# Taking both parts of x as one 512-column operand in two of three expert blocks, and more error parts by adding transfers

## The chip, the cores and the metric

The kernel runs on one core of a Trainium2 chip. The metric is the device time of one execution in microseconds (us). The kernel before was run three times: 2606.54, 2606.63 and 2608.71 us, median 2606.63 us.

## The reference

The reference is a small network on 256 tokens of width 1024 in f32: an mLSTM layer and a latent-attention layer, each followed by a PEER layer, and then a block of two feed-forward layers around a mixing layer. The change lies in PEER, which stands twice in the network:

```python
def peer_ffn(x, w_q, sub_keys, u, v):
    q = (xt @ w_q).reshape(T, PEER_HEADS, 2, PEER_HALF)
    s = jnp.einsum('thcd,hcnd->thcn', q, sub_keys)
    s1, i1 = lax.top_k(s[:, :, 0], K); s2, i2 = lax.top_k(s[:, :, 1], K)
    ...                                     # the best 16 of the 256 sums, for each of 8 heads
    gates = jax.nn.softmax(top_s, axis=-1)
    ub = jnp.take(u, eb, axis=0)            # 16,384 experts of width 1024
    act = jax.nn.gelu(jnp.einsum('thkd,td->thk', ub, xb), approximate=False)
    vb = jnp.take(v, eb, axis=0)
    return jnp.einsum('thk,thkd->td', gb * act, vb)
```

The kernel does not gather. It computes gelu(u x) for all 16,384 experts and all tokens, multiplies with a gate matrix that is zero for the experts not chosen, and multiplies the product with v.

## The kernel before, in words

Precision. Each f32 operand of a matrix product is kept as two parts in a narrower format of TensorE: `hi` is the rounded value, `lo` what is left over. A product is three products: hi·hi, hi·lo and lo·hi. For the activations the two parts are `self.xT[0]` and `self.xT[1]`, two halves of one tile of 128 x 2 x 8 x 256 (partition, part, chunk of the width, token), made by `new_xT` (line 459).

Weights come as units of 128 x 1024 f32 (512 KB) in a fixed order, through `Stream`. `load` (line 265) fetches a unit into one of three raw buffers on SP's queue. `prep` (line 284) casts it on ScalarE into `hi` (line 449, or 295) and subtracts on VectorE to get `lo` (line 450). For the units named in `on_dma`, VectorE is spared: `begin` (line 301) lets ScalarE write -w, rounded to the narrower format (line 306), and a transfer of GpSimd's queue then adds w from memory to it (line 307), which leaves `lo`; `spare` gives two buffers in turn for that. Outside the stretch with lent buffers `begin` of unit i is issued while block i-3 is. `fill` (line 310) runs ahead of the products by three units.

PEER. After 16 units for the queries, the 128 expert blocks of a layer follow (`block`, line 940). Block b takes one unit of u: `cols_late` (line 494) issues 16 matmuls with the hi weights, 8 chunks times the two parts of x, and then 8 with the lo weights and x's hi part, all of 256 columns into one PSUM accumulator (four buffers). While block b is issued, `activate` (line 1047) is called for block b-1: ScalarE applies Gelu from PSUM, in two pieces: the tokens whose gates are already joined go to a side buffer (line 1053) and are multiplied in by VectorE (`joins`, line 1061), the other tokens go straight into `big` (line 1056).

Up to block 43 of each layer VectorE works beside the blocks at the selection of the experts. Behind that `Gates` takes over: it spreads 67 steps over the blocks that are left (`upto`, line 1704). A step makes one-hot rows on VectorE (lines 1667, 1668, 1671), TensorE multiplies them (16 matmuls for every two steps, line 1680), and VectorE multiplies the product into `big` in two instructions (lines 1691 and 1693).

Order. VectorE's instructions in this stretch stand in the order in which the code issues them (`in_order`); in block b that is: the lo part of unit b+2, the step, the joins of block b-2. The order on the other engines is set by the scheduler of the framework, with data dependencies and in most places the order of the code; line 306 is held in program order. Each layer lends four more raw buffers to the first 44 expert units (`SELECT`, line 925).

Of the kernel before, what the change touches and what calls it, by code (L numbers as in the profile page):

```python
# [14 lines left out]
AF = mybir.ActivationFunctionType  # L15
ALU = mybir.AluOpType
AX = mybir.AxisListType.X
PSUM = bass.MemoryType.PSUM

P = 128  # L20
D = 1024
S = 256
NT = S // P
KC = D // P
# [17 lines left out]
SELECT, LENT = 44, 4  # L42
# [312 lines left out]
class Net:  # L355
# [96 lines left out]
    def mm(self, ps, a, b, start, stop):  # L452

        mm = self.nc.tensor.matmul
        mm(ps, a[0], b[0], start=start, stop=False)  # L455
        mm(ps, a[0], b[1], start=False, stop=False)  # L456
        mm(ps, a[1], b[0], start=False, stop=stop)  # L457

    def new_xT(self, pool=None, tag="xT", chunks=KC, bufs=1):
        pool = pool or self.gp  # L460
        t = self.t(pool, [P, 2, chunks, S], tag, F32R, bufs=bufs)
        return t[:, 0], t[:, 1]

    def transpose_split(self, src, xT, ti, c0, n):
# [28 lines left out]
    def cols_late(self, ps, xT, unit):  # L493

        mm = self.nc.tensor.matmul
        w = [u.rearrange("p (k c) -> p k c", k=KC) for u in unit]
        steps = [(0, k, part) for k in range(KC) for part in range(2)] + [(1, k, 0) for k in range(KC)]
        for n, (of, k, part) in enumerate(steps):
            mm(ps[:, :S], w[of][:, k], xT[part][:, k], start=n == 0, stop=n == len(steps) - 1)  # L499

    def rows(self, xT, nk=KC, done=None, before=False, then=None):

        acc = self.acc()
        n = nk - self.w.rings[1].size if done else nk
        if done:
            self.w.tail_at(self.w.i + nk)
        if before:
            self.rows_head(acc, xT)
        if then:
            then()  # L510
        for k in range(TAIL if before else 0, n):
            self.rows_k(acc, xT, k, self.w.next(), k == 0, k == nk - 1)
        if done:
            self.rows_tail(acc, [(xT, k) for k in range(n, nk)], n == 0, done)
        return acc
# [371 lines left out]
    def peer(self, layer, gain):  # L887
        nc, v, tc = self.nc, self.nc.vector, self.tc
        mm = nc.tensor.matmul
        with tc.tile_pool(name="pr", bufs=1) as pool:  # L890
            big = self.t(pool, [P, P, S], "big")
# [19 lines left out]

            first = self.w.i + 16
            self.w.lend([self.room(big, n) for n in range(14, 14 + LENT)], range(first, first + SELECT))
            self.w.on_dma = set(range(self.w.i + 16 + 1, self.w.i + 16 + P - 8, 3))

            sc = self.scores_of(big)
            st = {}
# [20 lines left out]
            now, late = {"last": None, "start": None}, []  # L938

            def block(b):  # L940
                ps = self.pp.tile([P, 512], F32, tag="acc", name=self.nm("ub"), bufs=4)
                self.cols_late(ps, self.xT, self.w.next())
                gates, start = now["gates"], now["start"]
                if start is not None:
                    gates.upto(b - 1, Gates.STEPS / (P - 2 - start))
                elif spend(steps, 1.6):
                    inner.close()
                    gates.pool = inner.enter_context(tc.tile_pool(name="gt", bufs=1))
                    now["start"] = b
                if b == P - 2:  # L950
                    gates.rest(b - 1)
                self.joins(late)
                if now["last"]:
                    self.activate(big, gates, late, *now["last"])
                now["last"] = b, ps

            def s_first(i):
                s_query(i) if i < 16 else block(i - 16)
# [11 lines left out]
            with self.in_order():  # L970
                skew([s_first, lambda i: None, s_second], 18)
                for b in range(2, P):
                    block(b)
            gates = now["gates"]
# [69 lines left out]
    def scores_of(self, big):  # L1044
        return big[:, P - 16:, :].rearrange("p b t -> p (b t)").rearrange("p (i h n) -> p i h n", i=NT, h=16)

    def activate(self, big, gates, late, b, ps):

        nc = self.nc
        t0 = gates.tokens if gates else 0  # L1050
        if t0:
            y = self.t(gates.pool, [P, S], "gl") if b % 2 else gates.room
            nc.scalar.activation(y[:, :t0], ps[:, :t0], AF.Gelu)
            late.append((big[:, b, :t0], y[:, :t0]))
        if t0 < S:
            nc.scalar.activation(big[:, b, t0:], ps[:, t0:S], AF.Gelu)  # L1056

    def joins(self, late):
        while late:
# [660 lines left out]
def spend(steps, budget):  # L1720

    while budget > 0:
        c = next(steps, False)
        if c is False:
            return True
        if c is None:
            return False
        budget -= c
    return False
# [59 lines left out]
```

## Time and profile before

| | us |
|---|---|
| median of three runs | 2606.63 |
| the profiled execution, its own time | 2605.68 |
| its span, first to last instruction | 2603.9 |
| TensorE busy in the span | 2545.4 (98%) |
| VectorE busy | 1777.1 (68%) |
| ScalarE busy | 1311.4 (50%) |
| GpSimd busy | 259.7 (10%) |

The two PEER layers run their expert blocks at about 213 to 623 us and 1183 to 1592 us of the span. A matmul's busy time overlaps with that of the next; the pace of a sequence is read from the starts.

### The profile page before, as it was taken

The page shows a single profiled execution, that of the slowest core. Times are in us where ns is not written, and L with a number is a line of the kernel's source. Part 1 is how long each engine was busy: PE and PEld are TensorE (multiplying, and loading weights), DVE is VectorE, ACT ScalarE, POOL GpSimd, SP SyncE. Part 2 cuts the span into 40 slices and gives each one's busy share as a digit, 9 for nine tenths or more (in the row PEclk, how much of TensorE's full clock was granted, in tenths as well). Part 3 has the DMA queues.
Part 4 walks back from the last instruction along what each step waited for, and adds up shares of the span by engine and source line. Part 5 has one row for each costly group of instructions (what it writes and reads, how often), then busy time and mean ns, then how long its engine had stood idle before and what let it go on. Part 6 is the DMA issues. An engine that isn't in the chain of part 4 may idle for free. (4 is left out here: it accounts for less than half of the span.)

```text
span 2603.9 us, 42855 instructions
## 1 busy us (share of the span) xinstructions
PE 2545.4 (98%) x16706; PEld 2300.9 (88%) x16706; DVE 1777.1 (68%) x3244; ACT 1311.4 (50%) x1981; POOL 259.7 (10%) x227
## 2 busy tenths in 40 slices
PE   8999999999999998999999999999999999999999
PEld 6889999999888887889999998888878998987898
DVE  5878977787555567679977776555566547675654
ACT  4445555554444445546555554444445445564543
POOL 0562000000000003010000000000011003101000
PEclk9999999999999999999999999999999999999999
DMA  6357777786555565357877776555566645554653
GB/s 240 118 187 203 216 206 218 211 216 214 194 194 194 194 201 167 116 197 212 225 204 215 211 217 211 193 194 193 194 199 198 218 161 176 171 177 154 210 195 105
DMA packets 139195, 502.42 MB, mean 193 GB/s; under 512 B 15832, under 2 KB 16088, under 8 KB 138992
## 3 DMA queue, kind: packets, MB, share of 16 engines
q1 hardware_dynamic: 122832, 443.93, 51.0%
q0 software_dynamic: 15440, 54.64, 10.8%
q8 instruction: 131, 2.15, 0.3%
q10 hardware_dynamic: 720, 1.11, 0.1%
q14 instruction: 72, 0.59, 0.1%
HBM read 494.38 MB, written 5.24 MB: 192 GB/s over the span
## 5 line engine op out<-in xcount | busy, mean ns | idle before, releaser
L449 ACT CAST whi<-wraw 128x1024 fp32r<-128x1024 f32 x488 | 510.1, 1047 | 689.7 <-PE acc L556 312.3
L450 DVE TENSOR_TENSOR wlo<-wraw,whi 128x1024 fp32r<-128x1024 f32 x446 | 546.9, 1227 | 445.3 <-ACT whi L449 444.3
L499 PE MATMUL ub<-xT,whi 128*128 128x256 f32 x4096 | 538.1, 284 | 0.0
L556 PE MATMUL acc<-whi,xT 128*128 128x512 f32 x1816 | 510.3, 394 | 12.8 <-ACT whi L449 7.3
L499 PEld LDWEIGHTS ub<-xT,whi 128*128 128x128 f32 x4096 | 508.3, 191 | 0.0
L556 PEld LDWEIGHTS acc<-whi,xT 128*128 128x128 f32 x1816 | 342.5, 190 | 86.6 <-ACT xT L449 7.7
L450 DVE TENSOR_TENSOR morelo<-wraw,morehi 128x1024 fp32r<-128x1024 f32 (+1 forms) x214 | 261.7, 1227 | 118.8 <-ACT morehi L449 118.4
L449 ACT CAST morehi<-wraw 128x1024 fp32r<-128x1024 f32 (+1 forms) x227 | 236.8, 1047 | 183.2 <-DMA wraw<-in_wst 72.5
L556 PE MATMUL acc<-wlo,xT 128*128 128x512 f32 x908 | 284.1, 393 | 0.2 <-DVE wlo L450 0.2
L556 PE MATMUL acc<-morehi,xT 128*128 128x512 f32 x808 | 233.9, 390 | 0.0
L499 PE MATMUL ub<-xT,wlo 128*128 128x256 f32 x1408 | 200.1, 285 | 8.6 <-DVE wlo L450 8.1
L556 PEld LDWEIGHTS acc<-wlo,xT 128*128 128x128 f32 x908 | 172.8, 190 | 37.3 <-DVE wlo L450 0.9
L499 PEld LDWEIGHTS ub<-xT,wlo 128*128 128x128 f32 x1408 | 180.9, 191 | 13.4 <-DVE wlo L450 13.1
L556 PEld LDWEIGHTS acc<-morehi,xT 128*128 128x128 f32 x808 | 151.2, 188 | 31.4 <-ACT morehi L449 0.5
L450 POOL TENSOR_TENSOR wlo<-wraw,whi 128x1024 fp32r<-128x1024 f32 (+1 forms) x42 | 100.7, 2400 | 707.0 <-ACT whi L449 702.0
L455 PE MATMUL ps<-xT,whi 128*128 128x256 f32 (+1 forms) x552 | 159.1, 289 | 0.0
L456 PE MATMUL ps<-xT,whi 128*128 128x256 f32 (+1 forms) x552 | 157.4, 285 | 0.4 <-DVE xT L450 0.4
L457 PE MATMUL ps<-xT,wlo 128*128 128x256 f32 (+1 forms) x552 | 157.0, 285 | 0.0
L307 POOL DMA_DIRECT2D x<-in_wst x80 | 69.0, 863 | 735.3 <-ACT big L1056 246.4
L556 PE MATMUL acc<-morelo,xT 128*128 128x512 f32 x404 | 128.3, 390 | 0.8 <-DVE morelo L450 0.8
L457 PE MATMUL ps<-xT,morelo 128*128 128x256 f32 x416 | 118.6, 285 | 1.9 <-POOL morelo L450 1.7
L456 PE MATMUL ps<-xT,morehi 128*128 128x256 f32 x416 | 118.4, 285 | 0.0
(498 smaller groups left out, 4160.0 us busy)
## 6 DMA issues: line engine op xcount, KB each, us to landing
wraw<-in_wst SPq DMA_DIRECT2D x768, 512.0 KB, 4.0
x<-in_wst POOLq DMA_DIRECT2D x80, 512.0 KB, 7.2
big<-in_wst SPq DMA_DIRECT2D x48, 512.0 KB, 5.4
wraw<-in_wst SPq DMA_DIRECT2D x10, 384.0 KB, 3.4
sp<-x SPq DMA_DIRECT2D x4, 512.0 KB, 3.0
big<-in_keys POOLq DMA_DIRECT2D x8, 256.0 KB, 7.0
sp<-big SPq DMA_DIRECT2D x4, 512.0 KB, 8.1
x<-sp POOLq DMA_DIRECT2D x4, 512.0 KB, 3.9
```

The source lines that it names most:

```text
L307: k.nc.gpsimd.dma_start(out=lo[:, :w], in_=self.src[i, :, :w], accum_op=ALU.add)
L449: self.nc.scalar.copy(hi, src)
L450: (self.nc.gpsimd if pool else self.nc.vector).tensor_tensor(lo, src, hi.bitcast(F32), op=ALU.subtract)
L455: mm(ps, a[0], b[0], start=start, stop=False)
L456: mm(ps, a[0], b[1], start=False, stop=False)
L457: mm(ps, a[1], b[0], start=False, stop=stop)
L499: mm(ps[:, :S], w[of][:, k], xT[part][:, k], start=n == 0, stop=n == len(steps) - 1)
L556: mm(acc[ti][h], a, w[b][:, h * 512:(h + 1) * 512], start=first, stop=last)
```

## The change

In blocks beside the gates (`start is not None`) whose number is no multiple of three, `cols_both` takes both parts of x for a chunk as one moving operand of 2 x 256 columns: 8 matmuls of 512 columns with the hi weights, then the 8 of 256 columns with the lo weights. The accumulator then holds hi·hi + lo·hi in its first 256 columns and hi·lo in the other 256. VectorE adds the halves with a reduction over an axis of two, into the place where Gelu's result will stand, and ScalarE's Gelu works in place there. The set `on_dma` keeps every third unit in the first 44 and names every second one from there to unit 118.

```diff
     def new_xT(self, pool=None, tag="xT", chunks=KC, bufs=1):
         ...
+        if tag == "xT":
+            self.both = t
         return t[:, 0], t[:, 1]
+    def cols_both(self, ps, unit):
+        mm = self.nc.tensor.matmul
+        w = [u.rearrange("p (k c) -> p k c", k=KC) for u in unit]
+        for k in range(KC):
+            mm(ps, w[0][:, k], self.both[:, :, k], start=k == 0, stop=False)
+        for k in range(KC):
+            mm(ps[:, :S], w[1][:, k], self.xT[0][:, k], start=False, stop=k == KC - 1)
...
-            self.w.on_dma = set(range(self.w.i + 16 + 1, self.w.i + 16 + P - 8, 3))
+            self.w.on_dma = set(range(first + 1, first + SELECT, 3)) | set(range(first + SELECT, first + P - 8, 2))
...
-                self.cols_late(ps, self.xT, self.w.next())
                 gates, start = now["gates"], now["start"]
+                both = start is not None and b % 3 != 0
+                if both:
+                    self.cols_both(ps, self.w.next())
+                else:
+                    self.cols_late(ps, self.xT, self.w.next())
...
-                now["last"] = b, ps
+                now["last"] = b, ps, both
...
-    def activate(self, big, gates, late, b, ps):
+    def activate(self, big, gates, late, b, ps, both):
         nc = self.nc
         t0 = gates.tokens if gates else 0
+        def gelu(dst, t):
+            src = ps[:, t]
+            if both:
+                src = dst
+                nc.vector.tensor_reduce(dst, ps.rearrange("p (a t) -> p t a", a=2)[:, t], axis=AX, op=ALU.add)
+            nc.scalar.activation(dst, src, AF.Gelu)
         if t0:
             y = self.t(gates.pool, [P, S], "gl") if b % 2 else gates.room
-            nc.scalar.activation(y[:, :t0], ps[:, :t0], AF.Gelu)
+            gelu(y[:, :t0], slice(0, t0))
             late.append((big[:, b, :t0], y[:, :t0]))
         if t0 < S:
-            nc.scalar.activation(big[:, b, t0:], ps[:, t0:S], AF.Gelu)
+            gelu(big[:, b, t0:], slice(t0, S))
```

## Rows read from the trace of the kernel before

**Rows 1.** Windows: busy us per engine, granted clock, DMA share, GB/s; selection, gates.

```profile
214.00:362.00 148.00, 143.76 (x1184) 141.34 (x1184) 134.95 (x407) 87.72 (x129) 12.94 (x15) 1.00 0.77 212
362.00:592.00 230.00, 228.62 (x2128) 227.18 (x2126) 173.72 (x341) 122.91 (x231) 19.89 (x23) 1.00 0.80 217
```

**Rows 2.** TensorE's waits in 214 to 362 us: total, times, longest.

```profile
PE ub L499 <- DVE wlo L450: 4.0, 8, 0.7
```

**Rows 3.** Timeline of TensorE beside the gates: start us, us, engine, line, operation.

```profile
464.18 2.08 PE L499 MATMUL ub<-xT,whi 128*128 128x256 f32 x16
466.10 1.12 PE L499 MATMUL ub<-xT,x 128*128 128x256 f32 x8
...
475.70 1.12 PE L499 MATMUL ub<-xT,x 128*128 128x256 f32 x8
...
591.97 2.16 PE L499 MATMUL ub<-xT,whi 128*128 128x256 f32 x16
```

**Rows 4.** Timeline of TensorE in the first layer: matmuls of 512 columns.

```profile
13.49 1.07 PE L556 MATMUL acc<-whi,xT 128*128 128x512 f32 x4
14.39 0.61 PE L556 MATMUL acc<-wlo,xT 128*128 128x512 f32 x2
14.85 1.07 PE L556 MATMUL acc<-whi,xT 128*128 128x512 f32 x4
```

**Rows 5.** Costliest groups of the page: busy us, mean ns of one, idle before.

```profile
L556 PE MATMUL acc<-whi,xT 128*128 128x512 f32 x1816 | 510.3, 394 | 12.8 <-ACT whi L449 7.3
L556 PEld LDWEIGHTS acc<-whi,xT 128*128 128x128 f32 x1816 | 342.5, 190 | 86.6 <-ACT xT L449 7.7
...
L307 POOL DMA_DIRECT2D x<-in_wst x80 | 69.0, 863 | 735.3 <-ACT big L1056 246.4
```

**Rows 6.** Tile ub, one row: Gelu of the joined tokens, odd blocks.

```profile
L1053 ACT ACTIVATE gl<-ub x82: 165/274/387, 360.9 to 1592.9; 128x256 f32<-128x256 f32 x4, 128x4 f32<-128x4 f32 x2, 128x8 f32<-128x8 f32 x2, 128x16 f32<-128x16 f32 x2
```

**Rows 7.** Groups by form on VectorE: reductions that read PSUM.

```profile
L756 DVE TENSOR_REDUCE m<-ps 128x1 f32<-128x256 f32 x8 | 3.3, 414 | 0.0
...
L756 DVE TENSOR_REDUCE m<-ps 128x1 f32<-128x128 f32 x8 | 2.2, 272 | 0.0
```

**Rows 8.** Timeline of VectorE beside the gates.

```profile
523.50 1.22 DVE L450 TENSOR_TENSOR wlo<-wraw,whi 128x1024 fp32r<-128x1024 f32 x1
524.64 0.55 DVE L1691 SCALAR_TENSOR_TENSOR big<-ps,big 128x384 f32<-128x384 f32 x1
525.11 0.28 DVE L1693 TENSOR_SCALAR big<-ps 128x128 f32<-128x128 f32 x1
525.30 0.68 DVE L1667 TENSOR_TENSOR hot<-x,idx 128x1024 f16<-128x1024 f16 x1
```

**Rows 9.** Window of the last third beside the gates, columns as in rows 1.

```profile
520.00:592.00 72.00, 72.00 (x674) 71.60 (x673) 57.64 (x110) 38.83 (x74) 6.05 (x7) 1.00 0.82 220
```

**Rows 10.** DMA in 362 to 592 us: packets, MB, share of 16 engines; issues.

```profile
q1 hardware_dynamic: 10170, 37.07, 48.4%
q0 software_dynamic: 3442, 12.53, 31.1%
...
wraw<-in_wst SPq DMA_DIRECT2D x70, 512.0 KB, 4.4
```

**Rows 11.** Timeline of ScalarE beside the gates.

```profile
464.68 1.06 ACT L306 ACTIVATE x<-wraw 128x1024 fp32r<-128x1024 f32 x1 [0.22 <-DMA wraw<-in_wst]
465.65 0.24 ACT L1053 ACTIVATE x<-ub 128x104 f32<-128x104 f32 x1
465.79 0.29 ACT L1056 ACTIVATE big<-ub 128x152 f32<-128x152 f32 x1
```

**Rows 12.** Timeline of GpSimd, one adding transfer; then line 307's landing time.

```profile
466.04 0.86 POOL L307 DMA_DIRECT2D x<-in_wst  x1 [9.06 <-ACT x L1053]
...
DMA to landing us min/median/max: 5.1/7.2/9.5
```

**Rows 13.** Waits of 362 to 592 us, one row: total, times, longest.

```profile
ACT x L306 <- DMA wraw<-in_wst: 13.6, 14, 3.4
```

## The prediction

> **What bounds the kernel now.** I read the windows by stage first, then TensorE's waits and its timeline, then VectorE, the DMA and the chain from raw weights to an added error part. Beside the gates TensorE is busy 228.62 of 230 us at full clock, VectorE 173.72 (76%), ScalarE 122.91 (53%), and the 16 DMA engines 0.80 [rows 1]. So TensorE sets the pace there, and only something that shortens its sequence, or makes it wait, moves the time. In the selection stretch ahead of it VectorE is busy 134.95 of 148 us (91%), and TensorE waits 4.0 us for error parts [rows 1, 2], 2.7% of the stretch: what a nearly full VectorE costs here, although its mean is under 100%.
>
> The blocks: 16 matmuls of 256 columns start in 1.92 us (464.18 to 466.10), so 0.120 us each and 2.88 us for 24 [rows 3]. Units whose error part comes by DMA stand at 466.10 and 475.70, three blocks apart. Unit 118, the last of them, begins at 591.97, which makes the block at 464.18 number 79: 39 blocks in 127.79 us, 3.277 us a block with its share of the gates' matmuls [rows 3].
>
> **Part 1, the 512-column matmuls.** In the first layer six matmuls of 512 columns start in 1.36 us (13.49 to 14.85), 0.2267 us each [rows 4]. The 256 columns more cost 106.7 ns, so of the 120 ns of a 256-column matmul 13.3 are a fixed part. It belongs to each matmul and not to a change of weights as far as the rows tell: the 512-column group has as many weight loads as matmuls, 1816 each [rows 5]. Eight pairs of 256 take 16 x 0.120 = 1.920 us, eight of 512 take 1.813; a block saves 0.107 us.
>
> How many blocks: Gelu into the side buffer on odd blocks comes 82 times, 41 a layer [rows 6], so the odd blocks 47 to 127 have joined tokens. The fourth of the 67 steps makes the first join; at 67/(126 - 43) = 0.807 steps a block it falls into block 48, where block 47 is activated. So `start` is 43, the new form can stand in blocks 44 to 127, 84 of them, of which 28 are multiples of three: 56 a layer, 112 in all. TensorE's sequence shortens by 112 x 0.107 = 11.95 us. Bounds: 11.95 us at best, nothing if a cost on the other engines eats it.
>
> The Trainium skill ("TensorE: Matmul & The Clock Gate", section "Wait — 56ns, not 53.3ns?") puts the fixed part of a warm matmul at about 2.5 ns. By that a block would save 8 x 2.5 = 0.02 us and the change 2.2 us, an estimate from that page; the trace shows 13.3 ns, and the sum goes by the trace. As a rival it stands below.
>
> **Part 2, the halves on VectorE.** Two reductions a block, 512 elements together. No row has an axis of two; nearest are the reductions from PSUM, 414 ns for 256 and 272 ns for 128 elements [rows 7]: 1.11 ns an element and 130 ns fixed, 0.83 us for both. What counts is start to start, about 0.08 us less than the duration: 1.14 for 1.22, 0.47 for 0.55, 0.19 for 0.28 [rows 8]. So 0.67 us, in two blocks of three: 0.447 us a block. Bounds: 0.57 us (512 x 1.11) to 0.83 us.
>
> **Part 3, more adding transfers.** The set had units 46, 49, ... 118 in this stretch, 25, and gets 44, 46, ... 118, 38; with the 15 ahead of it, which stay, the old set has 40 a layer, the 80 of the page [rows 5]. So 13 of 75 units lose VectorE's subtraction, 1.14 us: 0.197 us a block. ScalarE gains 13 times 1.06 us [rows 11], 14 us in 240, beside 47% idle; GpSimd 13 times 0.86 us, and it does nothing else there. The Gelu itself stays as long as it was to the bound of the rows: nothing on an engine half idle.
>
> VectorE then: 173.72/230 x 3.277 = 2.475 us a block now, 2.475 + 0.447 - 0.197 = 2.73 after; in the last third 57.64/72 x 3.277 = 2.62 now [rows 9], 2.87 after. TensorE's new block is 3.277 - 0.667 x 0.107 = 3.206. There is a new wait in its fixed order. A step's join at line 1691 reads block b-2 of `big`, whose Gelu now waits for a reduction that stands just ahead of it on VectorE. Where unit b+2 has its subtraction, 1.14 us lie between; where it comes by DMA, every second block, nothing does. There VectorE waits for the Gelu pair, 0.43 us (465.65 to 466.08 [rows 11]), and for what ScalarE has in hand, up to a cast or a line 306 of 1.06; I take 0.9 us in a third of the blocks (half of two thirds), 0.30 a block; bounds 0.14 (0.43 a time) and 0.85 (both 1.06 and the pair, 2.55). Behind the waiting join stand the makes for TensorE's gate products and the next subtractions and reductions. VectorE so needs 3.03 of 3.206 us in the mean (94%) and 3.17 in the last third (99%).
>
> The DMA: 48.4% of 230 us for 70.7 raw units (37.07 MB) is 1.574 us each, 31.1% for 23.9 adding transfers (12.53 MB) 2.99 us each [rows 10]. Per pair of blocks it now needs 2 x 1.574 + 2.99 = 6.14 us of TensorE's 6.41: 96%, where it is 80% now. The chain: line 306 starts at 464.68, the transfer at 466.04, lands 7.2 us later in the median, 9.5 at most [rows 11, 12], 473.2 or 475.5, and is wanted at 475.70 [rows 3]. The slack is 2.5 us, or 0.2 at the worst landing, and shrinks by three blocks' savings, some 0.2. A raw buffer that line 306 will read is now freed by a subtraction (unit i-3 is odd) and no longer by a cast; already line 306 waits for raw weights 14 times, 13.6 us [rows 13].
>
> **The sum.** Three resources stand at 94 to 100% with few buffers between them, so I charge a loss. The selection stretch is the row for it: 2.7% at a VectorE of 91%. I charge it where VectorE comes to 99%, the last 28 of the 84 blocks of each layer: 56 x 3.2 us x 2.7% = 4.8 us. Bounds: none, and 2.7% over all 168 blocks, 14.5 us. For the DMA I charge nothing in the likeliest case and keep it as a rival. So 2605.68 (the profiled execution) - 11.95 + 4.8 = 2598.5 us. The median of the runs lies 0.95 us above that execution; predicted is 2599.5 us, 7.1 us or 0.27% faster. Its own range is 2594.7 (no loss) to 2609.2 (loss everywhere). About 0.2%, 5.2 us, is what a measurement of this kernel can tell from no change.
>
> **The rivals.**
>
> VectorE takes over (slower). Mechanism: the wait of line 1691 for a Gelu that itself waits for VectorE. It decides once that wait passes 1.43 us in the mean, (3.206 - 2.73)/0.333, or 1.0 in the last third. At 2.0 us, between my 0.9 and the 2.55 of everything in its way, VectorE needs 2.73 + 0.333 x 2.0 = 3.40 us a block, 0.12 over the 3.277 of now: 168 x 0.12 = +20 us, 2627 us. For it: the order is fixed, and line 306 and casts of 1.06 us stand on ScalarE between. Against: ScalarE is idle half the time, and the scheduler may put the Gelu ahead of a cast.
>
> The DMA takes over. At 92% busy, a pair takes 6.14/0.92 = 6.67 us, 3.337 a block, +0.06 over 150 blocks: +9 us, less 1.3 for the twelve new blocks behind unit 118: 2614 us; at 96% it equals TensorE. For it: the raw loads and the transfers overlap already, and line 306 waits for raw weights. Against: the chain has 2.5 us of slack in the median.
>
> The shorter sequence isn't there, so that the change does not do what it says: if a 512-column matmul with new weights each time takes 0.240 us, the gain is nil, and the loss alone gives 2606.6 + 4.8 = 2611 us. Against it: the 0.2267 us, with a weight load each [rows 4, 5]. With the 2.2 us of the page named above it would be 2609 us.
>
> **How the numbers follow.** Likeliest case 0.60: 0.42 faster by over 0.2%, 0.18 within. VectorE 0.20: 0.18 slower, 0.02 within. DMA 0.14: 0.01 faster, 0.04 within, 0.09 slower. No gain 0.06: 0.03 within, 0.03 slower. Together 0.43 faster, 0.27 same, 0.30 slower. The range goes from 2594, just under the sum without loss, to 2624, into the VectorE case; about 0.12 is left out above and 0.04 below.
>
> **What would show it.** Part 1: groups of eight 512-column matmuls in the changed blocks, 1.81 us from the first to the first with lo weights, 896 in all; 0.24 apiece would prove that step wrong. Part 2: 224 reductions or a few less (pieces vanish where all or no tokens are joined), 0.4 us on the mean; VectorE near 83 to 88% of the stretch by busy time, and a new wait of line 1691 for line 1056 or 1053 of about 0.9 us, some 50 times. Part 3: 106 adding transfers, a DMA share near 0.95, landing within 8.5 us. TensorE's waits for `wlo`, for `ub` by DMA and for the one-hot rows should come to about 5 us. Waits of 15 us and over, and a block of 3.28 us or more, would make the prediction wrong; their releaser says which rival it was.

## The result, and the profile after

The changed kernel takes 2627.97 us (median of 7 runs, 2621.83 to 2635.22), the kernel before 2610.81 beside it (7 runs, 2606.54 to 2616.98): 1.0076 times as long, interval 1.0058 to 1.0095. It is slower, by about 20 us, where 2599.5 us was predicted. The profiled execution took 2627.97 us with a span of 2626.2, so 22.3 us more than that of before.

Most of it lies beside the gates. From the first matmul of the blocks to the first of the next projection (line 556, now 568) a layer took 411.26 and 410.00 us before and takes 418.79 and 420.05: the two stretches together 821.26, then 838.84, +17.6 us. These sums are called the block stretches below. The same window as in [rows 1], engines and columns as there:

```profile
362.00:592.00 230.00, 221.79 (x1718) 203.04 (x1716) 185.65 (x407) 132.57 (x241) 29.89 (x35) 1.00 0.89 236
```

TensorE, busy 228.62 us there before, is idle 8.21 us, all of it in waits for transfers. VectorE rises to 81% and the DMA to 0.89: neither is full. The wide matmuls stand as planned. TensorE's timeline of one changed block behind one of the old form (start, us, engine, line, operation):

```profile
381.52 2.08 PE L501 MATMUL ub<-xT,whi 128*128 128x256 f32 x16
383.44 0.76 PE L501 MATMUL ub<-xT,x 128*128 128x256 f32 x5
...
384.39 2.00 PE L509 MATMUL ub<-xT,whi 128*128 128x512 f32 x8
386.23 1.11 PE L511 MATMUL ub<-xT,wlo 128*128 128x256 f32 x8
```

Sixteen of 256 columns start in 1.92 us, 0.120 each as in [rows 3]; eight of 512 in 1.84, 0.230 each. A block saves 0.08 us and 112 blocks some 9.3 us. So the stretches lose not 17.6 us but 17.6 + 9.3 = 26.9. TensorE's waits, whole run (total, times, longest):

```profile
PE ub L511 <- DMA x<-in_wst: 8.7, 7, 2.7
PE ub L501 <- DVE wlo L450: 8.0, 16, 0.7
...
PE ub L501 <- DMA x<-in_wst: 6.3, 5, 2.0
...
PE acc L568 <- ACT x L449: 5.2, 2, 2.6
PE ps L1704 <- DVE hot L1695: 4.7, 7, 1.6
```

Before, these rows come to 0, 8.1, 1.4, 2.3 and 0 us. The named waits grow by 21 us of the 27; no row names the other 6. Most of these 6 can be the part of a wait that its row leaves out: the row of 0.48 us at 436.34 stands for matmuls that start 0.64 us behind their pace, and the eight that follow it start in 1.06 us instead of 0.95. Some 0.27 us for each of the 18 added waits for transfers and one-hot rows would make 5 us, an estimate from this wait and one of 1.71 us at 451.55. TensorE waits for added error parts, for one-hot rows, and at the end for the first operand of the next projection. What made those late stands in the waits of the other engines, 362 to 592 us:

```profile
ACT x L306 <- DMA wraw<-in_wst: 41.0, 15, 4.4
DVE big L1715 <- ACT big L1073: 30.6, 27, 3.3
...
ACT x L1073 <- DVE x L1072: 10.7, 9, 1.9
ACT gl L1073 <- DVE gl L1072: 9.4, 10, 2.1
DVE wlo L450 <- ACT whi L449: 9.4, 9, 1.9
```

Line 306 waited 13.6 us for raw weights before [rows 13], and the join (1691, now 1715) 4.3 for the Gelu, twice:

```profile
DVE big L1691 <- ACT big L1056: 4.3, 2, 3.5
```

One turn of what grew, first ScalarE's timeline, then VectorE's (in brackets the idle time before and its releaser):

```profile
442.17 1.06 ACT L306 ACTIVATE x<-wraw 128x1024 fp32r<-128x1024 f32 x1 [4.37 <-DMA wraw<-in_wst]
443.13 1.03 ACT L295 CAST whi<-wraw 128x1024 fp32r<-128x1024 f32 x1
444.06 0.26 ACT L1073 ACTIVATE x<-x 128x76 f32<-128x76 f32 x1
444.23 0.34 ACT L1073 ACTIVATE big<-big 128x180 f32<-128x180 f32 x1
```

```profile
431.97 1.21 DVE L450 TENSOR_TENSOR wlo<-wraw,whi 128x1024 fp32r<-128x1024 f32 x1
...
437.83 1.23 DVE L450 TENSOR_TENSOR wlo<-wraw,whi 128x1024 fp32r<-128x1024 f32 x1 [1.14 <-ACT whi L449]
...
440.98 0.31 DVE L1072 TENSOR_REDUCE x<-ub 128x76 f32<-128x152 f32 x1
441.20 0.52 DVE L1072 TENSOR_REDUCE big<-ub 128x180 f32<-128x360 f32 x1
444.60 0.45 DVE L1715 SCALAR_TENSOR_TENSOR big<-ps,big 128x284 f32<-128x284 f32 x1 [2.88 <-ACT big L1073]
...
447.29 1.22 DVE L450 TENSOR_TENSOR wlo<-wraw,whi 128x1024 fp32r<-128x1024 f32 x1
```

Read it as a ring. The reduction ends at 441.7, but the Gelu stands on ScalarE behind line 306, which waits until 442.17 for raw weights. The load of these was issued at 433.21, right behind the subtraction of 431.97, and landed 8.9 us later. The Gelu starts at 444.06; VectorE's next step has waited 2.88 us for it at its head. Behind that step stand the next one-hot rows, reductions and, at 447.29, the next subtraction, which frees a raw tile for a load that a later line 306 will wait for. Two subtractions lie 9.46 us apart here; every second block, they would be 6.4 apart. That the loads wait for subtractions above all shows in the waits of the load queue, 362 to 592 us, first the changed kernel's, then the one before's:

```profile
SPq L271 <- DVE wlo L450: 99.1, 29, 4.6
SPq L271 <- DMA wraw<-in_wst: 37.2, 26, 3.2
```

```profile
SPq L271 <- DVE wlo L450: 127.6, 38, 4.7
```

So a load waits for a subtraction in both kernels, and in the total even longer before. These rows show a link of the ring; they do not show that it grew. The transfers are longer too: in this window, from issue to landing, a raw load takes 6.5 us in the median (4.4 before [rows 10]) and an adding transfer 8.2 (7.3 before):

```profile
wraw<-in_wst SPq DMA_DIRECT2D x68, 512.0 KB, 6.5
x<-in_wst POOLq DMA_DIRECT2D x35, 512.0 KB, 8.2
```

Of the 22.3 us, 4.7 lie outside the stretches, some 3 of them right behind. At the switch to the next projection TensorE waits, and then runs at a lower granted clock (0.66, the third column from the right in the window row):

```profile
628.48 1.11 PE L511 MATMUL ub<-xT,wlo 128*128 128x256 f32 x8
632.19 0.75 PE L568 MATMUL acc<-whi,x 128*128 128x512 f32 x2 [2.60 <-ACT x L449]
```

```profile
632.00:637.00 5.00, 4.81 (x14) 3.81 (x15) 5.00 (x6) 2.60 (x5) 1.10 (x2) 0.66 0.38 116
```

Before, that wait was 1.13 us and the clock stayed at full speed. The lower of the two levels, 1.2 GHz, holds for some 3 us here and costs about 1.5 us a layer: the first 16 matmuls behind the wait start in 5.38 us, before in 3.84.

### The profile page after: what moved, and what is told of

It reads as the page before. It is cut to its first block, busy times and chain, and to the rows that moved or that the text cites. A ratio compares the mean times of both kernels' runs of the same rounds, so it can differ in the third digit from the quotient of the medians.

```text
span 2626.2 us, 41455 instructions
## 1 busy us (share of the span) xinstructions
PE 2542.0 (97%) x15810; PEld 2253.2 (86%) x15810; DVE 1819.2 (69%) x3434; ACT 1338.5 (51%) x2007; POOL 282.9 (11%) x253
## 3 DMA queue, kind: packets, MB, share of 16 engines
q0 software_dynamic: 19184, 68.27, 13.6%
## 5 line engine op out<-in xcount | busy, mean ns | idle before, releaser
L449 ACT CAST whi<-wraw 128x1024 fp32r<-128x1024 f32 (+1 forms) x462 | 482.6, 1046 | 559.5 <-PE acc L568 304.2
L450 DVE TENSOR_TENSOR wlo<-wraw,whi 128x1024 fp32r<-128x1024 f32 (+1 forms) x420 | 514.1, 1225 | 355.6 <-ACT whi L449 354.8
L501 PE MATMUL ub<-xT,whi 128*128 128x256 f32 x2304 | 301.8, 284 | 0.0
L501 PEld LDWEIGHTS ub<-xT,whi 128*128 128x128 f32 x2304 | 286.0, 191 | 0.0
L509 PE MATMUL ub<-xT,whi 128*128 128x512 f32 x896 | 228.2, 396 | 0.0
L509 PEld LDWEIGHTS ub<-xT,whi 128*128 128x128 f32 x896 | 160.5, 188 | 28.8
L307 POOL DMA_DIRECT2D x<-in_wst x106 | 91.4, 862 | 734.0 <-ACT big L1073 270.3
L306 ACT ACTIVATE x<-wraw 128x1024 fp32r<-128x1024 f32 x90 | 95.3, 1059 | 103.8 <-DMA wraw<-in_wst 100.6
```

Of the source, the lines that this page charges most:

```text
L306: k.tc.keep_in_program_order(k.nc.scalar.mul(lo[:, :w], self.raws[i][:, :w], -1.0))
L307: k.nc.gpsimd.dma_start(out=lo[:, :w], in_=self.src[i, :, :w], accum_op=ALU.add)
L449: self.nc.scalar.copy(hi, src)
L450: (self.nc.gpsimd if pool else self.nc.vector).tensor_tensor(lo, src, hi.bitcast(F32), op=ALU.subtract)
L509: mm(ps, w[0][:, k], self.both[:, :, k], start=k == 0, stop=False)
```

## The experiments

All were timed in five rounds beside the kernel before; a ratio of 0.0010 is 2.6 us. Expectations name theories by letters; each quote says what its letter claims.

**The two parts apart.** Four kernels set the new set of adding transfers against the wide matmuls with and without reductions.

e1_dma_only, the kernel before with the new set alone:

```
-  self.w.on_dma = set(range(self.w.i + 16 + 1, self.w.i + 16 + P - 8, 3))
+  self.w.on_dma = set(range(first + 1, first + SELECT, 3)) | set(range(first + SELECT, first + P - 8, 2))
```

> The kernel before with only the new set of adding transfers (every second unit behind the first 44); blocks and Gelu as before. Theory A, the chain raw weights, line 306, adding transfer comes late at this rate: TensorE waits for added error parts as in the changed kernel, about 5 us a layer by its rows, and nothing is saved, so +6 to +12 us on before. Theory B, VectorE's reductions are what costs and the added transfers only relieve VectorE: within 3 us of before or faster.

e2_both_only, the changed kernel with the old set (that line turned back):

> The changed kernel with the old set of adding transfers (every third unit). Theory A: without the late chain the 512-column matmuls pay, -9 us by their measured pace (0.083 us a block, 112 blocks), less a few us of waits for VectorE: -6 to 0 us on before. Theory B: VectorE has 0.2 us a block more than in the changed kernel and is overfull, so slower than the changed kernel: +22 to +45 us on before, with TensorE waiting for one-hot rows and subtractions.

e3_matmul_only, as e2 without the reductions, the Gelu reading the first half alone (hi·lo is left out in these blocks), and e4_matmul_dma, the same with the new set:

```
-            if both:
-                src = dst
-                nc.vector.tensor_reduce(dst, ps.rearrange("p (a t) -> p t a", a=2)[:, t], axis=AX, op=ALU.add)
```

> 512-column matmuls in the same blocks, old set of transfers, and no reductions: Gelu reads the first half of the accumulator alone, so the product of the hi weights with x's error part is left out in these blocks. It measures what the matmuls alone are worth: both theories -9 us (0.083 us a block by the changed kernel's trace, 112 blocks); -12 us if the 0.107 of the prediction holds.

> As the one without reductions (the product of the hi weights with x's error part is left out in two of three blocks beside the gates), but with the new set of transfers. Theory A: the late chain costs as much here as beside the reductions, so 8 to 18 us slower than the one with the old set, 0 to +9 us on before. Theory B: VectorE has room, so like the one with the old set, -9 us on before, within 3.

| kernel | ratio to before, interval | block stretches, us |
|---|---|---|
| e3: wide matmuls | 0.9975 (0.9962 to 0.9988) | 816.01 |
| e4: wide matmuls, new set | 0.9990 (0.9978 to 1.0002) | 819.69 |
| e1: new set | 1.0009 (0.9996 to 1.0021) | 826.3 |
| e2: wide matmuls, reductions | 1.0017 (1.0003 to 1.0031) | 824.58 |
| all three (the change) | 1.0076 (1.0058 to 1.0095) | 838.84 |

The stretches are those of the profiled execution alone, whose own time can lie some us beside the median: e1's, 2617.32 us, is the slowest of its twelve.

The wide matmuls alone save 6.5 us. The new set costs 2 to 4 us without reductions, neither of them clear of the intervals. The reductions cost 11 us with the old set (e2 less e3) and 22 with the new one (the change less e4). So neither part is the cause by itself: 11 us come only where both are. Of the expectations, e1 came out as theory B; e3 saved 6.5 us of the 9 expected; e2 (+4.4 us) and e4 (-2.6 us) fell between the two theories. The windows of 362 to 592 us, of e1, then e2, then e4:

```profile
362.00:592.00 230.00, 227.69 (x2119) 226.23 (x2118) 161.70 (x327) 132.99 (x242) 30.24 (x35) 1.00 0.94 243
```

```profile
362.00:592.00 230.00, 226.79 (x1764) 208.23 (x1763) 203.90 (x432) 125.76 (x234) 20.52 (x24) 1.00 0.79 215
```

```profile
362.00:592.00 230.00, 228.60 (x1758) 210.99 (x1759) 158.61 (x324) 132.69 (x243) 30.21 (x35) 0.99 0.94 242
```

A DMA share of 0.94 with TensorE busy 228.60 us (e4) shows that the transfers themselves fit where no reductions stand.

**Relief for VectorE on GpSimd.** f1_sub_on_pool is the changed kernel with the subtractions left beside the gates on GpSimd; f2_thirds has the old set and a third of the subtractions there.

```
+  self.w.on_pool.update(range(first + SELECT + 1, first + P - 8, 2))      # f1
+  self.w.on_pool.update(range(first + SELECT + 3, first + P - 8, 3))      # f2, with the old on_dma
```

> The changed kernel, with the subtractions that are left in units 45 to 119 of each layer on GpSimd in place of VectorE. The adding transfers are as many as in the changed kernel. Theory C, a loop: VectorE is late, so its subtractions free raw buffers late, so line 306 waits for raw weights and holds ScalarE's Gelus behind it, for which VectorE's join waits. VectorE loses 0.57 us a block, the loop opens, and most of the loss comes back: -9 to +3 us on before; line 306 waits under 40 us in all, the join under 20. Rival E, the load on the DMA engines (0.89 with twice the adding transfers) is what costs: +12 us or more on before, as the changed kernel.

> 512-column matmuls and reductions as changed, the old set of adding transfers (every third unit), and one third of the subtractions on GpSimd from unit 47 on; VectorE keeps one third. Theory C: VectorE has 0.38 us a block less than in the kernel with the old set and the reductions, so its +4 us turn into -9 to -4 us on before, the gain of the matmuls. Rival E: the same, for the DMA share is that of before; together with the run that has more transfers it tells the two apart.

Measured: 1.0139 (1.0116 to 1.0161) and 1.0206 (1.0189 to 1.0223), both slower still. VectorE was not relieved. In f1 its groups (line, operation, count; busy us, mean ns) are far longer beside GpSimd's subtractions, 685 ns becoming 974 to 1191:

```profile
L1696 DVE TENSOR_TENSOR hot<-x,gT 128x1024 f16<-128x1024 f16 x53 | 56.9, 1113 | 0.0
L1693 DVE TENSOR_TENSOR x<-x,idx 128x1024 f16<-128x1024 f16 x26 | 31.0, 1191 | 0.0
...
L1086 DVE TENSOR_TENSOR big<-x,big 128x160 f32<-128x160 f32 x1 | 2.5, 2524 | 0.0
```

```profile
L450 POOL TENSOR_TENSOR wlo<-wraw,whi 128x1024 fp32r<-128x1024 f32 x33 | 82.8, 2509 | 105.0 <-ACT whi L449 93.5 <-issue 11.5
```

So the two do not test the ring: their premise failed. Only this follows: f2 lost 54 us at a DMA share of 0.73, with TensorE waiting 28.1 us for transfers over the whole run, so a busy DMA is not needed for that.

**Line 306 behind the Gelu.** f3_begin_last is the changed kernel with line 306, and the transfer it starts, moved behind the Gelu of the same block, so that this Gelu no longer stands behind it.

```
+                self.w.hold = start is not None       # ahead of w.next(): begin nothing yet
 ...
+                self.w.hold = False                   # behind activate()
+                self.w.begin_due()
```

> The changed kernel, but beside the gates line 306 and its transfer are issued at the end of a block, behind the Gelus of the block ahead, and no longer in front of them. Theory C with ScalarE's order as the link: the join of VectorE waits under 30 us for Gelu in all, instead of 61, and the time is 8 to 15 us below the changed kernel. If the link is not ScalarE's order but VectorE's total work: within 4 us of the changed kernel, or slower, since the transfers start later and TensorE waits longer for them.

Measured: 1.0235 (1.0219 to 1.0251), +61 us. The join's waits did not go (26.1 us, 21 times, in 362 to 592 us; 69.6 over the whole run, where under 30 was expected), and TensorE waits for the transfers, now too late, over the whole run:

```profile
PE ub L506 <- DMA x<-in_wst: 35.3, 19, 3.1
PE ub L516 <- DMA x<-in_wst: 16.1, 12, 3.7
```

The transfers have no slack to give: line 306 has to stand early, here ahead of the Gelu. So f3 does not test the order on ScalarE by itself.

**Fewer reductions.** f4_one_of_three has the old set and the wide form in one block of three.

```
-                both = start is not None and b % 3 != 0
+                both = start is not None and b % 3 == 1
```

> Only blocks that leave 1 over three take the 512-column form (28 a layer), with the old set of transfers. These are the blocks whose error part comes by DMA. VectorE has 0.22 us a block on top, 2.70 of 3.25. Theory C: there is room, so the matmuls' part of the gain shows: -4.6 us at 0.083 us for 56 blocks, -5 to -1 us on before. Rival, each reduction costs wherever it stands: 0 to +3 us.

Measured: 1.0002 (0.9991 to 1.0012), block stretches 825.22. No gain: half the wide matmuls with half the reductions end within the measurement of before. That lies in the rival's range; the interval, -2.3 to +3.1 us on before, reaches into theory C's.

**Time or place.** g1_time_only lets the reductions write where nobody reads and the Gelu read PSUM; g2_order_only reduces 4 tokens only.

```
-                src = dst
-                nc.vector.tensor_reduce(dst, ps.rearrange("p (a t) -> p t a", a=2)[:, t], axis=AX, op=ALU.add)
+                nc.vector.tensor_reduce(self.dump, ps.rearrange("p (a t) -> p a t", a=2)[:, :, t], axis=AX, op=ALU.add)   # g1
+                nc.vector.tensor_reduce(dst[:, :4], ps.rearrange("p (a t) -> p t a", a=2)[:, t.start:t.start + 4], axis=AX, op=ALU.add)   # g2
```

> The changed kernel, but its two reductions write into a pair of numbers that nobody reads, and the Gelu takes the first half of the products from PSUM itself (left out: the high parts of the weights times x's error part, in the blocks concerned). VectorE has the same 0.65 us of reductions in such a block; ScalarE no longer waits for them. Theory T (VectorE's time): what costs is 0.65 us of VectorE per block, which makes its subtraction late, so that the raw tile comes free late and line 306 waits; the Gelu's wait is a symptom. Time as the changed kernel, +15 to +20 us on before; stretches of the blocks 835 to 840 us. Theory O (order): what costs is that the Gelu waits behind VectorE's step for the reduction, and that line 306 of the next block, which starts the adding transfer, stands behind that Gelu on ScalarE; the time alone is free beside TensorE. Time as the matmuls and transfers alone, -4 to 0 us; stretches about 820 us, the Gelu's waits on VectorE gone and line 306's waits back at some 36 us for 19.

> The changed kernel with reductions of 4 of the tokens instead of all, at the same place and into the tile that the Gelu writes; the Gelu reads PSUM behind them (left out: the high parts of the weights times x's error part, in the blocks concerned). VectorE's reductions shrink from 0.65 us to some 0.2 us in such a block (an estimate from the 272 ns of the short ones), the Gelu's wait behind VectorE's step stays. Theory T: a loss in proportion to the time, +2 to +6 us on before; stretches 820 to 826 us. Theory O: as the changed kernel, +15 to +20 us; stretches 833 to 840 us, with line 306 waiting about 100 us over the whole run.

Measured: 1.0416 (1.0395 to 1.0437), +108 us, and 1.0112 (1.0085 to 1.0140), +29 us. g1 missed both expectations; g2's time lies beyond both, while its stretches, 840.0 us, are those of theory O. The cause is in g1's waits, 362 to 592 us: the reductions now wait for the Gelu, as the two read the same products, one after the other.

```profile
DVE dump L1072 <- ACT x L1073: 26.2, 18, 4.0
...
DVE dump L1072 <- ACT gl L1073: 20.0, 20, 4.5
DVE big L1715 <- ACT big L1073: 18.2, 17, 3.9
```

g2 has the same new wait (40.0 us in its window), so neither isolates what it was made for. Still, g2's VectorE is busy only 163.59 of 230 us, less than before the change, and it loses at least as much as the change does. So VectorE's busy time is not what g2 lost; the new wait may be part of it.

**The place alone.** h_early_old and h_early_new make one reduction of all 256 tokens into the side tile, right behind the block's subtraction and ahead of the step, with the old and the new set. i_late_new is h_early_new with that reduction back behind the step.

```
                 (matmuls of block b, its subtraction)
+                if now["last"]:                                          # h_early: here
+                    now["last"] = self.add_early(gates, *now["last"])
                 ... gates.upto(...), self.joins(late)
                 if now["last"]:
+                    now["last"] = self.add_early(gates, *now["last"])    # i_late: here instead
                     self.activate(big, gates, late, *now["last"])
+    def add_early(self, gates, b, ps, both):
+        if both:
+            both = self.t(gates.pool, [P, S], "gl") if b % 2 else gates.room
+            self.nc.vector.tensor_reduce(both, ps.rearrange("p (a t) -> p t a", a=2), axis=AX, op=ALU.add)
...
```

> Wide matmuls and reductions with the set of adding transfers of before; the reduction is one of all 256 tokens, written to the side tile, and stands on VectorE right behind the block's subtraction and ahead of the selection's step, so that the Gelu finds its input earlier. Theory O: the loss against the matmuls alone shrinks from 12 us to 3 to 5 us, time -5 to -2 us on before; stretches 817 to 820 us, join waits under 5 us in 362 to 592 us. Theory T: VectorE has the same work less one fixed cost of some 0.1 us a block; time +1 to +4 us, stretches 822 to 825 us.

> The changed kernel with the reduction as one of all 256 tokens, written to the side tile, on VectorE right behind the block's subtraction and ahead of the selection's step. Theory O: the Gelu is no longer late and line 306 behind it neither; time -3 to +2 us on before, stretches 819 to 824 us, the join's waits on the Gelu under 10 us in 362 to 592 us (30.6 in the changed kernel). Theory T: +13 to +19 us; stretches 832 to 838 us, since VectorE's time in the loop is the same but for some 0.1 us a block.

> As h_early_new (one reduction of all 256 tokens into the side tile, the new set of adding transfers), but with the reduction behind the selection's step and the joins on VectorE, right ahead of the Gelu, where the change has its two. Theory O (the place): +14 to +20 us on before, stretches of the blocks 833 to 840 us, the join's waits on the Gelu back at 25 us or more in 362 to 592 us and line 306's at 40. Rival (two instructions and writing in place, not the place): +1 to +5 us, stretches 818 to 824 us as h_early_new.

| kernel | ratio to before, interval | block stretches, us |
|---|---|---|
| h_early_old | 0.9999 (0.9986 to 1.0011) | 817.53 |
| h_early_new | 1.0009 (0.9995 to 1.0023) | 819.4 |
| i_late_new | 1.0061 (1.0043 to 1.0078) | 841.45 |

h_early_new and i_late_new came out within or next to theory O's ranges, by time, stretches and waits, and far from their rivals'; h_early_old has theory O's stretches and waits, and a time between the two (-0.3 us). The place alone is worth 0.0052, 13.6 us; the profiled executions differ by 22 us in the stretches and by 16.0 in their own time. The window of h_early_new, then its waits in it, then both of i_late_new:

```profile
362.00:592.00 230.00, 228.98 (x1791) 211.30 (x1790) 191.85 (x377) 138.48 (x248) 29.35 (x34) 1.00 0.91 241
```

```profile
ACT x L306 <- DMA wraw<-in_wst: 16.8, 10, 3.7
...
DVE big L1723 <- ACT big L1079: 4.5, 6, 1.4
```

```profile
362.00:592.00 230.00, 222.92 (x1731) 204.43 (x1730) 182.44 (x361) 131.88 (x239) 29.57 (x35) 1.00 0.87 234
```

```profile
ACT x L306 <- DMA wraw<-in_wst: 42.1, 17, 5.8
DVE big L1722 <- ACT big L1078: 26.8, 25, 3.3
```

The same instructions, nearly the same engine shares, and both waits come back with the place. The faster of the two has the busier VectorE and the busier DMA. How the ring opens stands in h_early_new's timelines, VectorE's and then ScalarE's:

```profile
437.42 1.22 DVE L450 TENSOR_TENSOR wlo<-wraw,whi 128x1024 fp32r<-128x1024 f32 x1 [0.25 <-ACT whi L449]
438.56 0.68 DVE L1070 TENSOR_REDUCE x<-ub 128x256 f32<-128x512 f32 x1
439.16 0.44 DVE L1723 SCALAR_TENSOR_TENSOR big<-ps,big 128x280 f32<-128x280 f32 x1
...
441.96 0.44 DVE L1723 SCALAR_TENSOR_TENSOR big<-ps,big 128x284 f32<-128x284 f32 x1
```

```profile
437.50 1.06 ACT L306 ACTIVATE x<-wraw 128x1024 fp32r<-128x1024 f32 x1
439.34 0.27 ACT L1079 ACTIVATE x<-x 128x76 f32<-128x76 f32 x1 [0.77 <-DVE x L1070]
439.51 0.34 ACT L1079 ACTIVATE big<-x 128x180 f32<-128x180 f32 x1
```

The reduction is done at 439.24, the Gelu runs at 439.34 beside VectorE's step, and at the next step's head, at 441.96, its result has long been there.

What the runs show is the place: moved back behind the step, the same reduction costs 13.6 us and brings both waits back. That the loss runs round the whole ring, through the raw load, is read from single turns and from these waits; no run cut the ring at another link, by one more raw buffer for instance. Longer transfers by themselves are not the cause: h_early_new's take 6.5 and 8.1 us to land, as long as the changed kernel's.

**The price that is left.** i_early_all gives every block beside the gates the wide form, with early reductions:

```
-                both = start is not None and b % 3 != 0
+                both = start is not None
```

> As h_early_new, but every block beside the gates takes the wide matmuls and a reduction, not two of three: some 56 more of both. Theory O: with the reduction early, its time is hidden as long as VectorE has time left (192 of 230 us here, some 208 with the 16 more blocks by 0.69 us and what they displace), and TensorE saves 56 by 0.083 = 4.6 us more: -4 to +0 us on before, stretches 813 to 818 us. Rival (VectorE's time has its price in any place, 5 to 7 us for the first 112 reductions): +3 to +8 us, stretches 820 to 826 us.

Measured: 1.0052 (1.0034 to 1.0069), +13.5 us; block stretches 827.99 (417.22 and 410.77). Both expectations missed: the rival, that reductions cost even in the good place, had the direction and about half the size. VectorE is busy 88 and 91% in 362 to 592 and 1340 to 1592 us, and h_early_old, with 89 and 90%, loses nothing. TensorE's waits tell where the time went. At the switch to the next projection it waits 4.7 and 5.0 us for VectorE's last subtractions, where h_early_new waits 2.1 a layer. For added error parts it waits 9.0 us over the whole run, 4.3 in h_early_new. Two of these waits, of 3.76 and 2.37 us, stand in the first layer's stretch, each followed by a lower granted clock (0.57 in 363 to 367 and in 578 to 582 us). With 3.3 us more of idle time that makes most of the 6.4 us by which the first stretch is longer than the second. h_early_old's stretches are 3.7 us shorter than those of before and its time is not, but its profiled execution, 2601.63 us, is one of twelve that run from 2597.63 to 2610.85: the 3.7 us are within that spread. No version that does the whole computation was faster than the kernel before; h_early_old is level with it.

## Why the prediction was wrong

**The step that failed** is the loss: "so I charge a loss. The selection stretch is the row for it", 4.8 us, bounded by 14.5. Measured it is 26.9 us in the stretches and some 3 behind them; against e3, which has the wide matmuls and neither reductions nor new transfers, the change loses 0.0101, 26 us. The loss was sized by VectorE's share of time, and the share does not decide. With the same instructions VectorE is busy 79% of the window in i_late_new, which loses 0.0061, and 83% in h_early_new, which is level with before; at 89% h_early_old loses nothing. What decides is where the reduction stands, and by the traces the length of the ring subtraction, raw load, line 306, Gelu, step, subtraction. The row that sized the loss did not bear on it either: the eight waits of [rows 2] all stand at 251 to 319 us, ahead of the gates, and come back unchanged in the changed kernel (8.0 us in both layers, 8.1 before). The prediction named waits of 15 us and over as the sign of being wrong: those for `wlo`, for transfers and for one-hot rows came to 27.7 us where it put about 5.

**The new wait** was found, and nearly sized: 0.9 us in a third of the blocks was predicted, some 50 times; 60.7 us in 54 times were measured over the run, 1.12 us each. But its limit was worked out as if ScalarE had at most "a cast or a line 306 of 1.06" in hand. The row on record had already shown line 306 waiting for raw weights [rows 13]. That wait of up to 4.4 us stands ahead of the Gelu, and by the turn shown above it grows with the delay that the join's wait causes; no run measures this growth by itself. The prediction let the wait decide only from 1.43 us in the mean; the kernel was slower at 1.12.

**The rival** "VectorE takes over", 2627 us, had the place and the time (2627.97), at a chance of 0.20. Its price came out for another reason. It supposed VectorE short of time, needing 3.40 us a block; VectorE was idle 19% of the window, and i_late_new and h_early_new show that the order costs. That the time came so near its 2627 us is luck: it reckoned with 2.0 us a wait, and 1.12 were measured.

**Part 1.** 896 matmuls of 512 columns stand there, eight in 1.84 us and not 1.81. The saving is 0.08 us a block and not 0.107; over 112 blocks 9.3 us and not 11.95, of which e3 shows 6.5 in the time. The rate of [rows 4] came from groups in the first layer, and the saving, a small difference of two numbers, took the whole error. Nor could [rows 5] tell a fixed part of the matmul from one of its weight load, as both forms have one load for every matmul. The Trainium skill ("TensorE: Matmul & The Clock Gate", section "Wait — 56ns, not 53.3ns?") would have 2.5 ns saved for each pair made one; measured are 10.

**Part 2.** 216 reductions were made; those into `big` have a median of 429 ns (0.4 was predicted) and run next to each other at 0.67 us a block, as worked out. The size was right; "VectorE near 83 to 88%" came out at 81, as it stood idle in the waits.

**Part 3.** 106 adding transfers, as predicted; alone they cost some 2 to 4 us (e1, e4; not clear of the intervals) where nothing was charged. The DMA share is 0.89 and not 0.95, the median landing 8.2 us in the window; e1 and e4, in which TensorE hardly waits, do reach 0.94. The rival "the DMA takes over" falls as a cause by itself: h_early_new runs at 0.91, e4 at 0.94, with TensorE waiting 1.0 and 4.2 us for transfers in their windows. But the set matters together with the place. With it a raw tile that line 306 reads waits for a subtraction, as the prediction said and then did not price. That this makes the 11 us which only both parts together cost is argued, not shown; it fits that with the reduction early the two sets end 0.0010 apart, where with it late they end 0.0059 apart (e2 and the change).

**No gain in TensorE's sequence** falls with e3.

## What to carry to other kernels

When an instruction is put between two engines, follow the order on each until it comes back to where it started. If there is such a ring, its latency counts, and no engine's share of time will show it. A producer that another engine's in-order queue waits for belongs as early on its engine as its input allows: here the same reduction, one step earlier, gave back 13.6 us. And a saving that is a small difference of two measured rates should be measured in the very form in which it will run.

## What was not expected of the hardware

- Beside GpSimd's subtractions (2509 ns each), VectorE's f16 instructions of 1024 elements took 974 to 1191 ns in the mean instead of 685, and some f32 joins of up to 160 elements some 2.5 us: moving work to an idle GpSimd slowed the engine it was taken from.
- At the switch to the next projection the granted clock fell to 1.2 GHz for about 3 us behind TensorE waits of 2.60 us (the change) and 2.08 us (h_early_new). Behind waits of 1.13 us (before), 2.23 us (i_late_new) and 2.39 us (e2) at the same place it did not: the length of the wait alone does not decide it.
